# A reordered input projection: pooled inputs and values in the first pairs, the pooled path in eight steps, raw weights also in the tiles of the split of x

## The chip, the cores and the metric

The kernel runs on one core of one Trainium2 chip. The metric is the device time of one execution in microseconds (us). The engines are named as in the profile: PE is TensorE (PEld its weight loads), DVE is VectorE, ACT is ScalarE, POOL is GpSimd, SP is the engine that issues most DMAs. Each engine, and each engine's DMA queue, takes its instructions in order.

## The reference

One layer of a streaming encoder in float32, S = 1024 tokens, D = 1024, sandwich RMSNorms, input and output (1, 1024, 1024). What matters here is the first half:

```python
h = rms_norm(x, norm_mix_pre[l])
proj = h @ w_in[l]                       # 1024 x 4096: q, k, v, u (512 each), gates (2 x 1024)
q, k, v, u, gates = jnp.split(proj, splits, axis=-1)
y_a = chunk_band_attention(q, k, v, rel_bias[l]) @ w_attn_out[l]
y_b = multiscale_pool(u, w_pool_group[l], pool_scale[l]) @ w_pool_out[l]
g_a, g_b = jnp.split(jax.nn.sigmoid(gates + b_gate[l]), 2, axis=-1)
mix = (g_a * y_a + g_b * y_b) @ w_o[l]
x = x + rms_norm(mix, norm_mix_post[l])
f = conv_gated_ffn(rms_norm(x, norm_ffn_pre[l]), w_up[l], conv_w[l], conv_b[l], w_down[l])
x = x + rms_norm(f, norm_ffn_post[l])
```

`multiscale_pool` has four groups of 128 channels with trailing means over 2, 4, 8 and 16 tokens (computed by 1, 2, 3 and 4 doublings), minus the token, then a 128 x 128 matrix and a scale per channel. The FFN goes up to 2 x 2816, through a causal convolution of width 3, and down.

## The kernel before

A float32 operand is split into a high and a low part (`split`, L79: a cast on ACT gives `wh`, a subtraction on DVE gives `wl`), and each product is three matmuls of these parts (L85). A product of a 512 x 128 weight block with 512 tokens is twelve matmuls 128x512.

**In-projection (L367 to L738).** The 32 blocks of 128 output channels are computed in 16 pairs (`IN_PAIRS`), each by a Strassen-like scheme of seven products per pair of blocks (class `Pair`). It is done in two parts. First, while x still comes in, p1 and p2 of all pairs run on the tokens' first half (loop `for n in range(5, NP)`, with smaller weight loads `w12`); p1's results go to memory as `c1_d`. Then pairs are "turned" (`turn`): their whole raw weights are loaded (`load_win`, 1 MB, tile `win`), and `run_pair` runs p6, p3 and p7 of the pair, p5 of the next, and p4 of the pair. Per pair:

- four weight sums s1 (L203, `first`), s2, s4, s3 (L207 to L209, `sums`). The engine is the pair's `eng`: DVE for pairs 0 to 2, POOL for the others.
- `X_i<-c1b,R` on DVE (L254) seeds a bank; `u2` (L261) and `p5` (L218) are copies on ACT that hand a bank's content on.
- the evictions d(0,1) after p3 and d(1,1) after p7 are additions on DVE (L528); p4 cannot begin in p7's bank before d(1,1) has read it. d(0,0) and d(1,0) need no addition.
- `put` sends the result on: gates get their sigmoid on ACT (L521) and are stored by ACT's queue; pooled inputs u are stored to `u_d`; values wait in `vds` and are transposed by PE (`values`, `vps` L542, split into `vt`); q and k are split (`hl`, L499, L500) and stored.

**Pooled path.** `pooled_load` brings a group's u back as [128, 1024]. `pooled_path` (L554) does the doublings (`pl`, copies L560 and additions L561), the mean and the subtraction (L565 to L567) and the split into `pdh` (ACT) and `pdl` (DVE) at one place; `pooled_out` (L573), one pair later, loads and splits `wg`, makes the products `mxp` (six matmuls), scales them (`mo`) and splits into the tiles `mx`. In the kernel before the pooled groups are at pairs 6, 8, 10 and 12.

**Tiles.** "raw" has 6 buffers (raw weights, at first x, later `mx`), "S" and "o" 4 each, "hl" 2. x split in high and low (`XRh`, `XRl`) lies in tiles of the pool `hd` that attention's heads use later (tags `qk0`, `qk1`, `kl`, `bt`); p1 and p2 are its only readers.

**What follows.** `split_yb` loads and splits the first two weight blocks of the pooled out-projection during the last pair; then come that projection, attention, the out-projection and the FFN. The FFN's up-projection uses the same `Pair` class on 22 pairs u0 to u21 (`pair_up`, and `ahead` for u2 to u4, whose p1 and p2 run early); its sums are on POOL but for u5.

What sets the order: the program is written in the order of the loop; a scheduler then places each engine's instructions by priority (position in the program, raised by `tc.high_priority()`) and readiness. DMA queues take their issues in order.

Of the kernel before, what the change touches and what calls it, by code (L numbers as in the profile page):

```python
# [10 lines left out]
F32 = mybir.dt.float32  # L11
F32R = mybir.dt.float32r
AF = mybir.ActivationFunctionType
ALU = mybir.AluOpType
# [3 lines left out]
P = 128  # L18
S = 1024
# [15 lines left out]


IN_PAIRS = (
    [(16 + m, 24 + m) for m in range(4)]
    + [(12, 13), (14, 15)]
    + [(8, 9), (10, 11)]  # L40
    + [(16 + m, 24 + m) for m in range(4, 8)]
    + [(0, 4), (1, 5), (2, 6), (3, 7)]
)

# [2 lines left out]
def trunk(ctx, tc, xn, xt, w_first, w_in, cols, gain_pre, bias, w_ao, w_pg, w_po, w_o, gains, w_up, w_dn, out):  # L47
    nc = tc.nc
# [26 lines left out]
    def raw_tile(name):  # L75
        return rawp.tile([P, 2048], F32, tag="raw", name=name)
# [290 lines left out]
    with ExitStack() as ph:  # L367
# [4 lines left out]
        raws = {}  # L372

        def load_win(pi):
            raws[pi] = raw_tile(f"win{pi}")
            nc.sync.dma_start(raws[pi], w_in[pi])

        def half_tile(name):
# [2 lines left out]
        def out_tile(f, dt=F32):  # L381
            return tmp.tile([P, 512], dt, tag="hl", name=f)
# [117 lines left out]
                V.scalar_tensor_tensor(lo, src, scale, hi.bitcast(F32), ALU.mult, ALU.subtract)  # L500
            eng.dma_start(dst.rearrange("a p n -> p a n"), d.bitcast(F32))

        vds = []

        def put(fb, f, t, d, src):

# [17 lines left out]
        def evict_in(fb):  # L524
            def evict(f, t, ps, add):
                d = half_tile(f"d{fb[f]}_{t}")
                if add is not None:
                    V.tensor_tensor(d, ps, add, ALU.add)  # L528
                elif fb[f] < 16:
                    A.copy(d, ps)  # L530
                if (f, t, fb) == (1, 1, IN_PAIRS[-4]):

                    A.activation(warm, d[:, :1], AF.Exp, scale=0.0)
                put(fb, f, t, d, ps if add is None else d)
            return evict
# [13 lines left out]
        def pooled_load(m):  # L549
            u = tmp.tile([P, S], F32, tag="o", name=f"u{m}", bufs=4)  # L550
            nc.sync.dma_start(u, u_d[m])
            return u

        def pooled_path(m, u):  # L554
            w = POOL_WINDOWS[m]
            src = u
            step = 1
            while step < w:
                dst = tmp.tile([P, S], F32, tag="o", bufs=4, name=f"pl{m}_{step}")
                V.tensor_copy(dst[:, :step], src[:, :step])  # L560
                V.tensor_tensor(dst[:, step:], src[:, step:], src[:, :S - step], ALU.add)  # L561
                src = dst
                step *= 2
            e = w - 1
            V.tensor_tensor(src[:, :e], src[:, :e], cv[:, C_INV:C_INV + e], ALU.mult)  # L565
            V.tensor_tensor(src[:, :e], src[:, :e], u[:, :e], ALU.subtract)
# [4 lines left out]
            return m, hi, lo  # L571

        def pooled_out(m, hi, lo):  # L573
# [12 lines left out]

        first_yb = []

        def split_yb(m):
            wr = tmp.tile([P, 4, P], F32, tag="S", name=f"wr_yb{m}", bufs=4)  # L590
            (G if m else nc.sync).dma_start(wr, w_po[m])
            first_yb.append(split_w(wr, f"yb{m}", V))

        pairs = []

        def begin(n):
            p = Pair(None, T, psp, tmp, f"i{n}", None, 6, V if n < 3 else G)
# [114 lines left out]
        pair.p4(False)  # L714
        third.p5()
        nxt.p4(False)
        pair, pd = third, None
        for pi in range(2, NP):
            fb = IN_PAIRS[pi]
            for n in (pi + 1, pi + 2):  # L720
                if n < NP and n not in raws and (pi < 9 or n == pi + 1):
                    load_win(n)
            if pi in (7, 11):
                for x in range(2):
                    mx[x].append(rawp.tile([P, 2, S], F32R, tag="raw", name=f"mx{x}{pi}"))
            m = {6: 0, 8: 1, 10: 2, 12: 3}.get(pi)
            u = None if m is None else pooled_load(m)
            after = turn(pi + 1) if pi + 1 < NP else None
            run_pair(pair, after,
                     {"p6": lambda: split_yb(0), "p7": lambda: split_yb(1)} if after is None else (), True)  # L730
            pair = after
            values()
            if pd is not None:
                pooled_out(*pd)
            pd = None if u is None else pooled_path(m, u)
            if pi == 14:
                load_head(0)
                load_head(1)  # L738


    atp = ExitStack()
# [386 lines left out]
    with ExitStack() as ph:  # L1128
# [21 lines left out]

        def pair_up(g):

            return Pair(raws[g], Tu, psp, tmp, f"u{g}", evict_up(g), 4, V if g == 5 else G)

        def operand(name, src):
            hi, lo = Tu[name] = [Tp.tile([P, 4, 512], F32R, tag=name + x, name=name + x) for x in "hl"]
# [8 lines left out]

        def ahead(g):

            p = Pair(None, Tu, psp, tmp, f"u{g}", None, 4)
            w = Tp.tile([P, 1024], F32, tag=("T3h", "T3l", "T4h")[g - 2], name=f"w12_{g}")
            nc.sync.dma_start(w, w_up[g][:, :1024])  # L1170
            p.begin(w, p.pt("p1"))

            def evict(f, t, ps, add):
                d = p.pt("p2")
                A.copy(d, ps)
                nc.sync.dma_start(e_d[0, g - 2], d)
# [348 lines left out]
```

## Time and profile before

| | |
|---|---|
| runs | 1257.35, 1259.21, 1260.66 us; median 1259.21 |
| profiled execution | 1259.18 us, its span 1257.4 us |
| PE busy | 1231.3 us, 98% |
| DVE busy | 932.1 us, 74% |
| ACT busy | 663.5 us, 53% |
| POOL busy | 300.5 us, 24%, 236 instructions |

The span is cut into 40 slices in the page; the busy tenths of PE and DVE and PE's clock:

```profile
PE   8999999998899999999999999999999999999997
DVE  4897336758588877854799877676666676899968
PEclk9999999999999999999999999999999999999999
```

A slice is 31.4 us. The in-projection takes slices 1 to 11 (to about 345 us), attention follows, the FFN's up-projection begins at about 620 us. In slices 10 and 11 PE has 8. A timeline row gives start, duration, engine, line, operation, names (out<-in), sizes, and in brackets the engine's idle time before it with what ended it; a row of waits gives total, times and longest; a row of groups gives count | busy time, mean ns | idle time.

### The profile page before, as it was taken

The page shows a single profiled execution, that of the slowest core. Times are in us where ns is not written, and L with a number is a line of the kernel's source. Part 1 is how long each engine was busy: PE and PEld are TensorE (multiplying, and loading weights), DVE is VectorE, ACT ScalarE, POOL GpSimd, SP SyncE. Part 2 cuts the span into 40 slices and gives each one's busy share as a digit, 9 for nine tenths or more (in the row PEclk, how much of TensorE's full clock was granted, in tenths as well). Part 3 has the DMA queues.
Part 4 walks back from the last instruction along what each step waited for, and adds up shares of the span by engine and source line. Part 5 has one row for each costly group of instructions (what it writes and reads, how often), then busy time and mean ns, then how long its engine had stood idle before and what let it go on. Part 6 is the DMA issues. An engine that isn't in the chain of part 4 may idle for free.

```text
span 1257.4 us, 16281 instructions
## 1 busy us (share of the span) xinstructions
PE 1231.3 (98%) x5732; PEld 1021.9 (81%) x5732; DVE 932.1 (74%) x1497; ACT 663.5 (53%) x1170; POOL 300.5 (24%) x236
## 2 busy tenths in 40 slices
PE   8999999998899999999999999999999999999997
PEld 6888887787688998888888788888888888888886
DVE  4897336758588877854799877676666676899968
ACT  5664434544477774433464555555555454444553
POOL 0001433416244456000003443333333310000000
PEclk9999999999999999999999999999999999999999
DMA  9978423536787646512333332221221215902003
GB/s 334 322 245 310 142 101 108 215 119 228 235 291 266 207 150 253 204 68 84 118 121 143 128 136 97 95 101 51 101 101 43 101 67 204 390 17 101 34 1 135
DMA packets 63794, 193.85 MB, mean 154 GB/s; under 512 B 6048, under 2 KB 6688, under 8 KB 58592
## 3 DMA queue, kind: packets, MB, share of 16 engines
q1 hardware_dynamic: 55568, 176.29, 40.1%
q10 hardware_dynamic: 7056, 12.59, 2.7%
q0 software_dynamic: 1088, 3.93, 0.8%
q8 instruction: 45, 0.74, 0.2%
q14 instruction: 37, 0.30, 0.1%
HBM read 139.84 MB, written 52.95 MB: 153 GB/s over the span
## 4 chain that ended last, share of the span: by engine, by line
PE 82%; DVE 12%; issue 3%; ACT 2%; DMA 2%; SPq 0%; DVEq 0%; POOL 0%; ACTq 0%
PE X_u L85 16%; PE X_i L85 10%; PE Y_u L85 8%; PE X L85 7%; PE wops L1080 7%; PE Y_i L85 7%; PE Z_u L85 4%; PE y L85 4%; PE Y L85 3%; PE ybp L85 3%; PE f L881 3%; PE tp L856 2%; PE first L452 2%; PE Z_i L85 2%; DVE hc L1204 1%
## 5 line engine op out<-in xcount | busy, mean ns | idle before, releaser
L1204 DVE SCALAR_TENSOR_TENSOR hc<-hu,cv,hc 128x1022 f32<-128x1022 f32 (+1 forms) x88 | 120.1, 1366 | 30.2 <-ACT hc L1199 29.8
L79 ACT CAST wh_u<-s_u 128x512 fp32r<-128x512 f32 x88 | 54.3, 618 | 86.3 <-PE Y_u L85 43.5
L79 DVE TENSOR_TENSOR wl_u<-s_u,wh_u 128x512 fp32r<-128x512 f32 x88 | 65.4, 746 | 34.0 <-ACT wh_u L79 34.0
L79 ACT CAST wh_i<-s_i 128x512 fp32r<-128x512 f32 x64 | 39.6, 621 | 73.2 <-PE Y_i L85 21.3
L79 DVE TENSOR_TENSOR wl_i<-s_i,wh_i 128x512 fp32r<-128x512 f32 x64 | 50.2, 791 | 35.5 <-ACT wh_i L79 35.5
L203 POOL TENSOR_TENSOR s_i<-win 128x512 f32<-128x512 f32 x13 | 23.7, 1821 | 174.5 <-DVE wl_i L79 134.9
L79 ACT CAST wh_u<-wup 128x512 fp32r<-128x512 f32 x60 | 37.2, 621 | 48.7 <-PE X_u L85 25.8
L1199 ACT ACTIVATE hc<-hu,cv 128x1024 f32<-128x1024 f32 x44 | 54.7, 1244 | 10.8 <-DVE hu L1148 9.9
L207 POOL TENSOR_TENSOR s_u<-s_u,wup 128x512 f32<-128x512 f32 x19 | 27.1, 1425 | 133.5 <-DVE wl_u L79 122.5
L203 POOL TENSOR_TENSOR s_u<-wup 128x512 f32<-128x512 f32 x19 | 34.0, 1791 | 72.9 <-DVE wl_u L79 72.9
L835 POOL TENSOR_SCALAR pe<-pe,st 128x640 f32<-128x640 f32 (+4 forms) x58 | 40.7, 705 | 44.0 <-DVE st L833 29.6
L79 DVE TENSOR_TENSOR ptl<-tp,pth 128x512 fp32r<-128x512 f32 (+3 forms) x80 | 42.8, 552 | 7.8 <-ACT pth L79 7.2
L831 ACT ACTIVATE pe<-sm,st 128x640 f32<-128x640 f32 (+2 forms) x64 | 44.3, 694 | 7.7 <-DVE st L829 7.5
L1209 ACT ACTIVATE hc<-hc 128x1024 f32<-128x1024 f32 x22 | 23.4, 1063 | 45.5 <-DVE hc L1204 45.5
L209 POOL TENSOR_TENSOR s_u<-wup 128x512 f32<-128x512 f32 x19 | 40.1, 2110 | 26.5 <-DVE wl_u L79 26.5
L79 ACT CAST pth<-tp 128x512 fp32r<-128x512 f32 (+3 forms) x80 | 36.3, 475 | 15.9 <-PE tp L856 11.0
L79 DVE TENSOR_TENSOR wl_u<-wup,wh_u 128x512 fp32r<-128x512 f32 x60 | 43.2, 721 | 0.7
L85 PE MATMUL ybp<-mx,wh_yb 128*128 128x512 f32 x128 | 43.4, 412 | 0.0
L829 DVE CUSTOM_DVE_ANT_0 sm<-pst,bt 128x640 f32<-128x640 f32 (+2 forms) x64 | 40.7, 652 | 3.1 <-issue 1.7
L881 PE MATMUL f<-pth,vv 128*128 128x256 f32 x144 | 36.5, 286 | 0.0
L881 PE MATMUL f<-ptl,vv 128*128 128x256 f32 x144 | 36.5, 287 | 0.0
L856 PE MATMUL tp<-ident,pe 128*128 128x128 f32 x240 | 35.4, 275 | 0.2
(518 smaller groups left out, 4158.7 us busy)
## 6 DMA issues: line engine op xcount, KB each, us to landing
wup<-in_w_up SPq DMA_DIRECT2D x22, 1024.0 KB, 5.0
win<-in_w_in SPq DMA_DIRECT2D x16, 1024.0 KB, 5.5
g_d<-hc SPq DMA_DIRECT2D x20, 512.0 KB, 2.6
a<-g_d SPq DMA_DIRECT2D x8, 1024.0 KB, 10.9
b<-in_w_dn SPq DMA_DIRECT2D x8, 1024.0 KB, 12.8
sig_d<-d ACTq DMA_DIRECT2D x28, 256.0 KB, 2.4
w<-in_w_in SPq DMA_DIRECT2D x12, 512.0 KB, 6.8
x<-in_xn SPq DMA_DIRECT2D x8, 512.0 KB, 8.5
```

The costliest lines, as they stand in the source:

```text
L79: return A.copy(hi, src), (eng or V).tensor_tensor(lo, src, hi.bitcast(F32), ALU.subtract)
L85: nc.tensor.matmul(ps, a[i], b[i], start=start and i == 0 and p == 0, stop=stop and i == n - 1 and p == 2, skip_group_check=True,)
L203: self.eng.tensor_tensor(self.s1, self.w21, self.w22, ALU.add)
L209: self.eng.tensor_tensor(self.s3, self.w11, self.w21, ALU.subtract)
L829: V.tensor_tensor_reduce(so, sv, bv, -1.0, 3e38, ALU.add, ALU.min, st[:, 0:1])
L831: A.activation(pe[:, :n], sm[:, :n], AF.Exp, scale=-1.0, bias=st[:, 0:1], accum_out=st[:, 1:2])
L835: (V if 4 * h + J in (0, 1, 31) else G).tensor_scalar(pe[:, :n], pe[:, :n], st[:, 2:3], 1.0, ALU.mult, ALU.mult)
L856: nc.tensor.transpose(tp[:, c * P:(c + 1) * P], pe[:, b * P:(b + 1) * P], ident)
L881: nc.tensor.matmul(fo, vv[:, kb, e].rearrange("p a d -> p (a d)"), t[:, s], start=s == slots[0] and x == 0, stop=s == slots[-1] and x == 1)
L1080: nc.tensor.matmul(ps[:, 512 * c:512 * c + 512], a[k // 4][:, k % 4, sl], wo[k][b][:, 512 * c:512 * c + 512], start=k == 0 and x == 0, sto ...
L1199: A.activation(c, hu, AF.Identity, scale=cv[:, C_CW + 88 + b:C_CW + 89 + b], bias=cv[:, C_CB + b:C_CB + b + 1])
L1204: V.scalar_tensor_tensor(c[:, n:], hu[:, :S - n], cv[:, w:w + 1], c[:, n:], ALU.mult, ALU.add)
```

## The change

Four things are changed.

1. The order of pairs: pooled inputs, values, all gates, then q and k.
2. The pooled path is cut into steps (`pooled_sums`, `pooled_split`, `pooled_out`) which are put at the ends of pairs 4 to 11, one or two per pair, each issued behind the pair's eviction d(1,1); that eviction gets high priority.
3. The raw weights of pairs 6, 8, 10 and 12 go into the tiles of the split of x (`qk0`, `qk1`), so that weights are always loaded two pairs ahead. The loads for `split_yb` go to SP and stand, with the loads of heads 0 and 1, before the last pair.
4. Weight sums: DVE for pairs 3 to 11 (POOL before; nine pairs with four sums each), and in the FFN for u2, u3, u4 and u6 (sixteen sums).

```diff
 IN_PAIRS = (
-    [(16 + m, 24 + m) for m in range(4)]
-    + [(12, 13), (14, 15)]
+    [(12, 13), (14, 15)]
     + [(8, 9), (10, 11)]
-    + [(16 + m, 24 + m) for m in range(4, 8)]
+    + [(16 + m, 24 + m) for m in range(8)]
     + [(0, 4), (1, 5), (2, 6), (3, 7)]
 )
...
         def load_win(pi):
-            raws[pi] = raw_tile(f"win{pi}")
+            if pi in (6, 8, 10, 12):
+                raws[pi] = hd.tile([P, 2048], F32, tag=f"qk{pi // 2 % 2}", name=f"win{pi}")
+            else:
+                raws[pi] = raw_tile(f"win{pi}")
             nc.sync.dma_start(raws[pi], w_in[pi])
...
                 if add is not None:
-                    V.tensor_tensor(d, ps, add, ALU.add)
+                    with tc.high_priority() if f == t == 1 else nullcontext():
+                        kept[f, t] = V.tensor_tensor(d, ps, add, ALU.add)
...
-        def pooled_path(m, u):
-            w = POOL_WINDOWS[m]
-            src = u
-            step = 1
-            while step < w:
+            pooled[m] = u, u, 1
+
+        def pooled_sums(m, end):
+            u, src, step = pooled[m]
+            while step < end:
                 dst = tmp.tile([P, S], F32, tag="o", bufs=4, name=f"pl{m}_{step}")
                 V.tensor_copy(dst[:, :step], src[:, :step])
                 V.tensor_tensor(dst[:, step:], src[:, step:], src[:, :S - step], ALU.add)
                 src = dst
                 step *= 2
+            pooled[m] = u, src, step
+
+        def pooled_split(m):
+            w = POOL_WINDOWS[m]
+            pooled_sums(m, w)
+            u, src, _ = pooled[m]
...
-        first_yb = []
+        first_yb, wr_yb = [], []
+
+        def load_yb(m):
+            wr_yb.append(out_tile(f"wr_yb{m}").rearrange("p (k c) -> p k c", k=4))
+            nc.sync.dma_start(wr_yb[m], w_po[m])
 
         def split_yb(m):
-            wr = tmp.tile([P, 4, P], F32, tag="S", name=f"wr_yb{m}", bufs=4)
-            (G if m else nc.sync).dma_start(wr, w_po[m])
-            first_yb.append(split_w(wr, f"yb{m}", V))
+            first_yb.append(split_w(wr_yb[m], f"yb{m}", V))
...
-            p = Pair(None, T, psp, tmp, f"i{n}", None, 6, V if n < 3 else G)
+            p = Pair(None, T, psp, tmp, f"i{n}", None, 6, V if n < 12 else G)
...
+        steps = {
+            4: lambda: pooled_split(0),
+            5: lambda: (pooled_out(0), pooled_sums(1, 4)),
+            6: lambda: pooled_split(1),
+            7: lambda: (pooled_out(1), pooled_sums(2, 4)),
+            8: lambda: pooled_split(2),
+            9: lambda: (pooled_out(2), pooled_sums(3, 8)),
+            10: lambda: pooled_split(3),
+            11: lambda: pooled_out(3),
+        }
         for pi in range(2, NP):
...
-                if n < NP and n not in raws and (pi < 9 or n == pi + 1):
+                if n < NP and n not in raws:
                     load_win(n)
-            if pi in (7, 11):
+            if pi in (5, 9):
...
-            m = {6: 0, 8: 1, 10: 2, 12: 3}.get(pi)
-            u = None if m is None else pooled_load(m)
+            if pi in (4, 5, 7, 9):
+                pooled_load({4: 0, 5: 1, 7: 2, 9: 3}[pi])
             after = turn(pi + 1) if pi + 1 < NP else None
+            if after is None:
+                load_yb(0)
+                load_yb(1)
+                load_head(0)
+                load_head(1)
             run_pair(...)
...
-            if pd is not None:
-                pooled_out(*pd)
-            pd = None if u is None else pooled_path(m, u)
-            if pi == 14:
-                load_head(0)
-                load_head(1)
+            if pi in steps:
+                with tc.issue_after(kept[1, 1].ins):
+                    steps[pi]()
...
         def pair_up(g):
-            return Pair(raws[g], Tu, psp, tmp, f"u{g}", evict_up(g), 4, V if g == 5 else G)
+            return Pair(raws[g], Tu, psp, tmp, f"u{g}", evict_up(g), 4, V if g < 7 else G)
...
         def ahead(g):
-            p = Pair(None, Tu, psp, tmp, f"u{g}", None, 4)
+            p = Pair(None, Tu, psp, tmp, f"u{g}", None, 4, V)
```

DVE around d(1,1) beside the sums of pooled group 3, first before, in the turn of pair 13 (the result for block 5, a k block; d5_1 is its d(1,1)). The numbers in the names `i13`, `pl3_4` are the pair, and the group with its doubling; the last number of a name is the buffer's.

```order
L561 TENSOR_TENSOR pl3_4_2577<-pl3_2_2574 128x1020
L528 TENSOR_TENSOR d1_1_2632<-Y_i13_2530,u2_i13_2596 128x512
L560 COPY pl3_8_2580<-pl3_4_2577 128x8
L561 TENSOR_TENSOR pl3_8_2580<-pl3_4_2577 128x1016
L528 TENSOR_TENSOR d5_1_2654<-X_i13_2597,p5_i13_2531 128x512
L565 TENSOR_TENSOR pl3_8_2580<-pl3_8_2580,cv_76 128x15
L567 SCALAR_TENSOR_TENSOR pl3_8_2580<-pl3_8_2580,u3_2453 128x1009
L566 TENSOR_TENSOR pl3_8_2580<-pl3_8_2580,u3_2453 128x15
```

And now, in the turn of pair 10 (a gate pair; the lines are the changed file's, d30_1 is the d(1,1)):

```order
L533 TENSOR_TENSOR d22_1_2286<-Y_i10_2175,u2_i10_2250 128x512
L78 TENSOR_TENSOR wl_6_i11_2374<-s2_i11_2310,wh_6_i11_2373 128x512
L533 TENSOR_TENSOR d30_1_2306<-X_i10_2251,p5_i10_2176 128x512
L563 COPY pl3_8_2354<-pl3_4_2241 128x8
L564 TENSOR_TENSOR pl3_8_2354<-pl3_4_2241 128x1016
L78 TENSOR_TENSOR wl_3_i11_2391<-s4_i11_2311,wh_3_i11_2390 128x512
L574 TENSOR_TENSOR pl3_8_2354<-pl3_8_2354,cv_76 128x15
L576 SCALAR_TENSOR_TENSOR pl3_8_2354<-pl3_8_2354,u3_2103 128x1009
```

The last doubling has moved from between the two evictions to behind both, and three pairs earlier in the program.

ACT around the cast `pdh` of pooled group 1, before, in the turn of pair 9:

```order
L521 ACTIVATE d28_0_2043<-X_i8_1943,cv_76 128x512
L522 DMA sig_d_70<-d28_0_2043 128x512
L79 CAST pdh1_2055<-pl1_2_2049 128x1024
L261 COPY u2_i9_2063<-X_i9_2064 128x512
L79 CAST wh_4_i9_2148<-win9_1778 128x512
```

And now, in the turn of pair 6:

```order
L525 DMA sig_d_70<-d26_1_1784 128x512
L78 CAST pdh1_1835<-pl1_2_1719 128x1024
L217 COPY p5_i7_1795<-Y_i7_1794 128x512
L78 CAST wh_7_i7_1887<-s3_i7_1790 128x512
L78 CAST wh_5_i8_1915<-s1_i8_1845 128x512
```

What stands behind the cast is now the copy of p5 and no longer that of u2.

SP's queue around the load of the first block for `split_yb`, before; the second block was on POOL's queue:

```order
L362 DMA kl1_2855<-k_d_67 64x1024
L501 DMA k_d_67<-hl_2795 128x2x512
L591 DMA wr_yb0_2882<-in_w_po 128x512
L786 DMA vv0_3009<-v_d_68 128x2x1024
L798 DMA sgb0_2987<-sig_d_70 128x1024
```

And now:

```order
L379 DMA win14_2496<-in_w_in 128x2048
L601 DMA wr_yb0_2846<-in_w_po 128x512
L632 DMA c1b_14_2616<-c1_d_74 128x512
L601 DMA wr_yb1_2848<-in_w_po 128x512
L504 DMA q_d_66<-hl_2540 128x2x512
L356 DMA qk0_2850<-q_d_66 128x1024
```

Both blocks stand ahead of the first stores of q and k, where before the one load came behind the last of them.

More of the change, by code (lines that the diff above doesn't have):

```diff
@@ L501, in store_split @@
             eng.dma_start(dst.rearrange("a p n -> p a n"), d.bitcast(F32))
-        vds = []
+        vds, kept = [], {}
         def put(fb, f, t, d, src):
@@ L551, in pooled_load @@
             nc.sync.dma_start(u, u_d[m])
-            return u
-        def pooled_path(m, u):
-            w = POOL_WINDOWS[m]
-            src = u
-            step = 1
-            while step < w:
+            pooled[m] = u, u, 1
+        def pooled_sums(m, end):
+            u, src, step = pooled[m]
+            while step < end:
                 dst = tmp.tile([P, S], F32, tag="o", bufs=4, name=f"pl{m}_{step}")
@@ L570, in pooled_path, with pooled_out @@
             split(hi, lo, src)
-            return m, hi, lo
-        def pooled_out(m, hi, lo):
+            pooled[m] = hi, lo
+        def pooled_out(m):
+            hi, lo = pooled.pop(m)
             wg = tmp.tile([P, P], F32, tag="S", bufs=4, name=f"wg{m}")
@@ L716, in trunk @@
         nxt.p4(False)
-        pair, pd = third, None
+        pair, pooled = third, {}
+        steps = {
[8 more added lines that the diff above has]
+        }
         for pi in range(2, NP):
-            fb = IN_PAIRS[pi]
             for n in (pi + 1, pi + 2):
-                if n < NP and n not in raws and (pi < 9 or n == pi + 1):
+                if n < NP and n not in raws:
                     load_win(n)
-            if pi in (7, 11):
+            if pi in (5, 9):
                 for x in range(2):
                     mx[x].append(rawp.tile([P, 2, S], F32R, tag="raw", name=f"mx{x}{pi}"))
-            m = {6: 0, 8: 1, 10: 2, 12: 3}.get(pi)
-            u = None if m is None else pooled_load(m)
+            if pi in (4, 5, 7, 9):
+                pooled_load({4: 0, 5: 1, 7: 2, 9: 3}[pi])
             after = turn(pi + 1) if pi + 1 < NP else None
+            if after is None:
[3 more added lines that the diff above has]
+                load_head(1)
             run_pair(pair, after,
```

## The prediction

> **What bounds the kernel now.** I read the busy shares and the chain of the page first, then the waits of TensorE (PE) for the stage that the change rewrites, then windows of that stage, then single rows around each wait.
>
> ```profile
> PE 1231.3 (98%) x5732; PEld 1021.9 (81%) x5732; DVE 932.1 (74%) x1497; ACT 663.5 (53%) x1170; POOL 300.5 (24%) x236
> PE 82%; DVE 12%; issue 3%; ACT 2%; DMA 2%; SPq 0%; DVEq 0%; POOL 0%; ACTq 0%
> 125.00:195.00 70.00, 70.00 (x311) 57.95 (x310) 27.03 (x41) 27.13 (x46) 28.67 (x21) 1.00 0.33 113
> 237.00:251.00 14.00, 14.00 (x55) 11.39 (x56) 10.43 (x15) 8.01 (x15) 7.75 (x5) 0.88 0.36 129
> 293.00:308.00 15.00, 12.28 (x51) 9.80 (x50) 15.00 (x20) 4.57 (x8) 8.10 (x5) 0.92 0.82 275
> 323.00:345.00 22.00, 18.46 (x76) 14.53 (x75) 9.35 (x18) 8.48 (x18) 3.41 (x11) 0.92 0.80 275
> ```
>
> A windows row is from:to, length, busy time (count) of PE, its weight load, DVE, ACT, POOL, then PE's granted clock, DMA share, GB/s. PE is the bound, and no matmul is added or removed, so only PE's idle time and its slow clock can be won: 1257.4 - 1231.3 = 26.1 us idle, plus what the clock costs inside busy time. From 125 to 195 us PE is full at clock 1.00. The losses stand where pooled path, values and gates meet, 195 to 345 us. PE's waits there (us in total, times, longest):
>
> ```profile
> PE Y_i L85 <- ACT wh_i L79: 3.5, 1, 3.5
> PE X_i L85 <- DVE d L528: 3.3, 2, 2.7
> PE X_i L85 <- ACT u_i L261: 2.5, 2, 2.0
> PE vps L542 <- DVE vt L79: 1.1, 1, 1.1
> PE Y_i L85 <- DVE wl_i L79: 0.8, 1, 0.8
> ```
>
> Together 11.2 us. After the three longest, twelve matmuls run partly at half clock; from the chain (start, us, piece), with an undisturbed product last:
>
> ```profile
> 236.84 4.61 PE X_i L85 x12
> 305.94 4.45 PE X_i L85 x12
> 332.47 4.78 PE Y_i L85 x12
> 244.20 2.72 PE X_i L85 x12
> ```
>
> The excess over 2.72 is 1.89 + 1.73 + 2.06 = 5.7 us. The pool from which this change can draw is 11.2 + 5.7 = 16.9 us. Why each happens:
>
> ```profile
> 235.26 1.04 ACT L79 CAST pdh<-pl 128x1024 fp32r<-128x1024 f32 x1 [4.74 <-DVE pl L566]
> 236.21 0.58 ACT L261 COPY u_i<-X_i 128x512 f32<-128x512 f32 x1
> 303.40 0.68 DVE L528 TENSOR_TENSOR d<-Y_i,u_i 128x512 f32<-128x512 f32 x1
> 304.00 0.16 DVE L560 COPY pl<-pl 128x8 f32<-128x8 f32 x1
> 304.07 1.21 DVE L561 TENSOR_TENSOR pl<-pl 128x1016 f32<-128x1016 f32 x1
> 305.20 0.68 DVE L528 TENSOR_TENSOR d<-X_i,p_i 128x512 f32<-128x512 f32 x1
> 331.28 0.62 ACT L79 CAST wh_yb<-wr_yb 128x512 fp32r<-128x512 f32 x1 [3.74 <-DMA wr_yb<-in_w_po]
> 283.35 1.29 POOL L203 TENSOR_TENSOR s_i<-win 128x512 f32<-128x512 f32 x1 [19.74 <-DMA win<-in_w_in]
> ```
>
> At 236.84 ACT's queue is held for 4.74 us by pooled group 1's cast, and the copy of u that PE waits for stands behind it. At 305.94 the sums of group 3 stand between and ahead of the two evictions d on a DVE that was busy for the whole 15 us (the window 293:308); d began at 305.20, long after its product. The shorter waits for d (0.6) and u (0.5) stand beside other groups' pooled work. At 332.47 the first weight block of the next projection was fetched too late. The 0.8 us is a weight sum that waited for its own raw weights.
>
> **The change, part by part.**
>
> (a) *Pooled path in eight steps, over gate pairs.* A turned pair is five products of 2.72, 13.6 us. From 125 to 195 us, 70/13.6 = 5.1 such pairs, DVE is busy 27.03, or 5.3 us a pair. To this come four weight sums from POOL; one more 128x512 operation holds DVE for 304.00 - 303.40 = 0.60, so 2.4. The heaviest step is group 2's output with the first three sums of group 3: three copies and adds at 305.20 - 304.00 = 1.20, 3.6, and three small operations, about 1.4. Sum 12.7 us, against 13.6 plus six matmuls of group 2 (half a product, 1.36): 15.0. It fits, though with little over. What decides is d(1,1), which must be finished while the next product runs, 2.72 us: it now has priority and the steps are issued behind it, so at worst one long operation (1.2) and its own 0.7 stand before it, 1.9 us. The cast pdh now stands ahead of the copy of p5 and not of u; the copy is needed only by the next d(1,1), four products later. Removed: 2.7 + 0.6 + 2.5 in waits, and 1.89 + 1.73 of clock: 9.4 us.
>
> (b) *Values in early pairs whose sums are on DVE.* The wait of 1.1 us before vps:
>
> ```profile
> 215.23 0.66 PE L542 MATMUL vps<-ident,d 128*128 128x128 f32 x4 [1.11 <-DVE vt L79]
> 212.19 0.69 DVE L79 TENSOR_TENSOR wl_i<-s_i,wh_i 128x512 fp32r<-128x512 f32 x1 [1.01 <-ACT wh_i L79]
> 212.80 1.79 DVE L254 TENSOR_TENSOR X_i<-c1b,R 128x512 f32<-128x512 f32 x1
> 212.28 1.75 POOL L209 TENSOR_TENSOR s_i<-win 128x512 f32<-128x512 f32 x1
> 195.00:223.00 28.00, 26.89 (x130) 21.78 (x129) 18.93 (x28) 14.60 (x26) 7.72 (x5) 1.00 0.44 156
> ```
>
> The DVE operation from 212.80 took 1.79, where the like one before it took 0.69, and ended 0.56 after POOL's sum ended (214.03): POOL's sum held it back 1.1 us, and vt behind it. Without POOL's sum that goes: 1.1. So a sum moved costs DVE 0.60 and takes away up to 1.1; net it costs between +0.60 and -0.5 each. I count it at nothing in the pairs, where DVE has idle time.
>
> (c) *The block's load and the raw weights.* The load wr_yb was issued at 324.26 and took 7.00:
>
> ```profile
> 324.26 7.00 DMA wr_yb<-in_w_po
> ```
>
> It now stands on SP's queue two to three pairs earlier, some 30 us ahead of need, into a tile of group 3's weights; behind it on SP wait the q and k stores and two head loads, and win15, which is needed a pair later (13.6 us, against some 7 for a load). That returns 3.5 + 2.06. Raw weights always two ahead return the 0.8.
>
> (d) *Function tables on ACT.* With gates no longer first, sigmoid falls between the squares and the root of the norm, so the table is loaded three times there and not once:
>
> ```profile
> 44.00 1.28 ACT L521 ACT_TABLE_LOAD   x1
> PE rps L471 <- DVE bc L468: 0.2, 1, 0.2
> ```
>
> Two more at 1.28 are 2.56 us on ACT. They delay the norm's root, and through DVE's bc PE's transposes rps; these already waited 0.2, but now stand one product later in PE's order. Bounds: 0 if that product (2.72) covers it, 2.56 if nothing does. I take 0.3, near the row's own 0.2.
>
> (e) *FFN up-projection, sixteen sums from POOL to DVE.*
>
> ```profile
> 640.00:700.00 60.00, 59.77 (x264) 49.13 (x263) 59.37 (x66) 32.28 (x46) 16.37 (x9) 1.00 0.45 158
> L1204 DVE SCALAR_TENSOR_TENSOR hc<-hu,cv,hc 128x1022 f32<-128x1022 f32 (+1 forms) x11 | 17.7, 1626 | 0.3
> L79 DVE TENSOR_TENSOR wl_u<-s_u,wh_u 128x512 fp32r<-128x512 f32 x16 | 12.9, 819 | 0.0
> L79 DVE TENSOR_TENSOR wl_u<-wup,wh_u 128x512 fp32r<-128x512 f32 x5 | 4.4, 899 | 0.0
> 695.17 1.27 DVE L1204 SCALAR_TENSOR_TENSOR hc<-hu,cv,hc 128x1023 f32<-128x1023 f32 x1
> PE X_u L85 <- DVE hu L1148: 1.0, 2, 0.8
> ```
>
> DVE is full there (59.37 of 60), so cover is gone and the price counts. Nine sums add 9 x 0.60 = 5.4 us. Against it: L1204 takes 1626 ns in the mean and 1.27 us undisturbed, 11 x 0.36 = 3.9; the two wl groups stand 0.13 and 0.21 over 0.69, 2.1 + 1.0. Up to 7.0 us of slowing, all beside POOL's sums, goes away. Net 1.6 us less for DVE. PE's waits there are 1.0 in all; I take back 0.3. Bounds: 1.0 won; or, with no slowing removed, 5.4 - 0.6 of DVE's idle time = 4.8 lost.
>
> **Sum.** 9.4 (a) + 1.1 (b) + 5.6 + 0.8 (c) = 16.9; I leave 1.0 of it as new short waits, since the heaviest step leaves only 2.3 us of DVE. Less 0.3 (d), plus 0.3 (e): 15.9. The profiled execution took 1259.18 us (span 1257.4); the median of the runs is 1259.21, practically the same, so the result stands for it: 1243.3, say 1243.5.
>
> One rule speaks against this sum. The Trainium skill, "TensorE: Matmul & The Clock Gate", Part 1, says that the clock falls to half after at least one idle window of about 3.4 us. By that rule only the wait of 3.5 could have cost clock, the 1.89 and 1.73 would have another cause and stay, and the sum would end at 1247. This trace disagrees: PE's granted clock fell after waits of 2.0 and 2.7 as well, and not after 1.1 (the window 195:223 has 1.00). I go by the trace: a wait of 2 us costs about 4. That the slow matmuls stay for another reason gets 0.05 of the forecast's chance below; 1243.5 + 3.6 = 1247 is its upper end.
>
> **Rivals.**
>
> 1. *DVE late in some steps* (0.13). The steps with three adds miss the 2.72 us. Each such stall costs what 305.94 did, 2.7 + 1.73 = 4.5. Two of eight: 1252.5. For it: DVE has no idle time from 293 to 308 today. Against: priority, and the sum of 12.7 in 15.0.
> 2. *Pooled stalls only move* (0.08): a cast or wgl now blocks another copy on ACT, as pdh did. Then (a) and (b) return nothing, (c) returns 6.4: 1253.
> 3. *FFN's DVE becomes the bound* (0.10): the moved sums cost 4.8 there, and the slowing stays because others of POOL's sums remain: 1243.5 + 0.3 + 4.8 = 1248.6.
> 4. *Slower* (0.06): d(1,1) late by 2 us or more in each step that ends with sums or a split. It decides from four stalls of 4.5 upward, 18 against the 15.9 won; six give 1243.5 + 27 = 1270. For it: a full DVE; against: between 125 and 195 us DVE is busy 39%.
>
> **How the numbers follow.** The forecast, 1240 to 1247, has 0.57: full return and 1.0 in the FFN give 1259.2 - 17.9 = 1241.3, and a little more with fewer slowed operations; 2.56 for the tables and another 1 of waits give 1247. The remaining 0.06 is for gains and losses that cancel, near 1257. What a measurement can tell is about 0.3%, 3.8 us: faster means below 1255.4. Forecast and rivals 1 to 3 lie there, 0.88; same 0.06; slower 0.06. The range that leaves out the slow cases and half of the odd ones is 1239.5 to 1254.
>
> **What would show it.** Right: PE's waits of 195 to 345 us are gone but for pieces below 1 us, PE's clock reads 1.00 from 31 us to the end of the in-projection, no idle ACT before wh_yb, POOL at about 52 sums fewer (236 instructions to about 184), the phase ending some 16 us earlier. Wrong in (a): a row X_i with idle time from d, and twelve matmuls over 4 us. Wrong in (d): PE waiting for bc by more than 0.5 near 53 us. Wrong in (e): X_u or Y_u waiting for hu or wl_u, summing over 2 us between 620 and 760.

## The result and the profile after

The changed kernel takes 1239.18 us (median of six runs, 1238.54 to 1240.40), the kernel before 1259.14 (six runs, 1257.35 to 1260.97). The ratio is 0.9842, interval 0.983 to 0.9855: 20.0 us faster. Forecast were 15.9 us, 1243.5, in a range from 1239.5: the direction was right, the gain a fifth too small, and the time lies just below the range. Of the eight runs of one experiment below, that with only the sums moved, one took 1535.56 us at a granted clock of 0.75; its time is the median of the seven others.

The page after, busy shares and shares of the chain:

```profile
PE 1222.6 (99%) x5732; PEld 1018.1 (82%) x5732; DVE 947.8 (77%) x1549; ACT 667.8 (54%) x1172; POOL 211.6 (17%) x183
PE 90%; DVE 7%; issue 1%; ACT 1%; DMA 0%; POOL 0%; DVEq 0%; SPq 0%; POOLq 0%; ACTq 0%
```

PE has the same 5732 matmuls. POOL issues 183 instructions in place of 236, DVE 52 more. The chain, of which DVE held 12%, is 90% PE. PE's waits from the start to 345 us, all of them:

```profile
PE first L455 <- ACT w0s L78: 6.3, 1, 6.3
PE rps L474 <- DVE bc L471: 0.2, 1, 0.2
PE tp L880 <- POOL pe L859: 0.2, 1, 0.2
```

The five rows of 11.2 us are gone, and nothing has come in their place. The windows of the two kernels, from 125 us to about the end of the in-projection, before first, and then the FFN's two windows after:

```profile
125.00:342.00 217.00, 205.87 (x890) 167.17 (x889) 125.52 (x174) 97.80 (x167) 80.07 (x53) 0.98 0.48 164
125.00:330.00 205.00, 205.00 (x919) 169.67 (x918) 143.11 (x226) 105.35 (x181) 28.62 (x28) 1.00 0.51 176
623.00:683.00 60.00, 60.00 (x266) 49.71 (x265) 59.31 (x78) 32.54 (x45) 0.00 (x0) 1.00 0.46 159
683.00:743.00 60.00, 60.00 (x266) 49.66 (x266) 50.74 (x57) 32.57 (x49) 11.49 (x8) 1.00 0.34 127
```

Before, PE idled 217.00 - 205.87 = 11.1 us at a mean clock of 0.98; after, it is full at 1.00. In the FFN, too, PE is full (60.00 twice, where it had 59.77 and 59.06), beside a DVE as busy as before: 59.31.

Adding up, from the starts of the matmuls, what lies beyond their usual spacing (0.227 us for 128x512), PE lost 18.2 us from 125 us to the end of the in-projection before and 0.2 after; in the 140 us of the FFN's first part 2.2 before and 0.1 after; from 31 to 125 us 0.4 before and 0.7 after. That is 18.0 + 2.1 - 0.3 = 19.8, the gain of the medians. (The two profiled spans differ by 20.4. Ahead of 31 us, where the first matmuls of each kernel are twice as far apart, PE lost 2.8 us before and 1.6 after.)

### The profile page after: what moved, and what is told of

The parts are those of the page before. It is cut to its first block, busy times and chain, and to the rows that moved or that the text cites. A ratio compares the mean times of both kernels' runs of the same rounds, so it can differ in the third digit from the quotient of the medians.

```text
span 1237.0 us, 16222 instructions
## 1 busy us (share of the span) xinstructions
PE 1222.6 (99%) x5732; PEld 1018.1 (82%) x5732; DVE 947.8 (77%) x1549; ACT 667.8 (54%) x1172; POOL 211.6 (17%) x183
## 4 chain that ended last, share of the span: by engine, by line
PE 90%; DVE 7%; issue 1%; ACT 1%; DMA 0%; POOL 0%; DVEq 0%; SPq 0%; POOLq 0%; ACTq 0%
PE X_u L84 19%; PE X_i L84 12%; PE Y_u L84 10%; PE Y_i L84 8%; PE X L84 7%; PE wops L1104 7%; PE Z_u L84 4%; PE y L84 4%; PE Y L84 4%; PE ybp L84 3%; PE f L905 2%; PE tp L880 2%; PE first L455 2%; PE Z_i L84 2%; DVE b L1394 1%; DVE a L1394 1%
## 5 line engine op out<-in xcount | busy, mean ns | idle before, releaser
L1228 DVE SCALAR_TENSOR_TENSOR hc<-hu,cv,hc 128x1022 f32<-128x1022 f32 (+1 forms) x88 | 115.5, 1314 | 27.8 <-ACT hc L1223 27.7
L78 DVE TENSOR_TENSOR wl_u<-s_u,wh_u 128x512 fp32r<-128x512 f32 x88 | 62.3, 711 | 33.9 <-ACT wh_u L78 33.9
L78 DVE TENSOR_TENSOR wl_i<-s_i,wh_i 128x512 fp32r<-128x512 f32 x64 | 44.7, 700 | 21.9 <-ACT wh_i L78 16.9
L202 POOL TENSOR_TENSOR s_i<-win 128x512 f32<-128x512 f32 x4 | 6.2, 1561 | 259.4 <-DVE wl_i L78 248.3
L202 POOL TENSOR_TENSOR s_u<-wup 128x512 f32<-128x512 f32 x15 | 25.7, 1713 | 139.3 <-DVE wl_u L78 139.3
L78 ACT CAST pth<-tp 128x512 fp32r<-128x512 f32 (+3 forms) x80 | 36.3, 475 | 15.9 <-PE tp L880 11.0
L206 POOL TENSOR_TENSOR s_u<-s_u,wup 128x512 f32<-128x512 f32 x15 | 19.4, 1293 | 102.3 <-DVE wl_u L78 99.6
L208 POOL TENSOR_TENSOR s_u<-wup 128x512 f32<-128x512 f32 x15 | 32.2, 2145 | 23.5 <-DVE wl_u L78 23.5
```

The lines of the kernel that those rows point to most:

```text
L78: return A.copy(hi, src), (eng or V).tensor_tensor(lo, src, hi.bitcast(F32), ALU.subtract)
L202: self.eng.tensor_tensor(self.s1, self.w21, self.w22, ALU.add)
L208: self.eng.tensor_tensor(self.s3, self.w11, self.w21, ALU.subtract)
L1228: V.scalar_tensor_tensor(c[:, n:], hu[:, :S - n], cv[:, w:w + 1], c[:, n:], ALU.mult, ALU.add)
```

## The experiments

Times are medians. Each experiment undoes one thing in the changed kernel, or does one thing in the kernel before; the last two measure DVE's room. The kernel before, on the same chip each time, took 1259.25 to 1259.61 us, and 1261.39 beside the last two, which were run once.

**FFN sums back on POOL.**

```diff
-            return Pair(..., evict_up(g), 4, V if g < 7 else G)
+            return Pair(..., evict_up(g), 4, V if g == 5 else G)
-            p = Pair(None, Tu, psp, tmp, f"u{g}", None, 4, V)
+            p = Pair(None, Tu, psp, tmp, f"u{g}", None, 4)
```

> The changed kernel with the FFN's sixteen weight sums back on POOL. Theory (the gain that the prediction missed lies partly in the FFN, where waits read as 1.0 us cost about 2): 1.7 to 2.3 us slower than the changed kernel's 1239.18, so about 1241, and waits of X_u for hu are back between 605 and 745 us. Rival (the FFN gave 0.3 as forecast, the rest is the clock at the start): 1239.2 to 1239.6.

Measured: 1241.42, ratio 0.986 (0.9845 to 0.9875), 2.2 slower than the changed kernel. Its waits of the FFN's first part, its window, and DVE's three groups of the changed kernel (623 to 683 us):

```profile
PE X_u L84 <- DVE hu L1172: 1.1, 2, 0.9
625.00:685.00 60.00, 59.76 (x264) 49.18 (x263) 59.37 (x66) 31.10 (x43) 18.52 (x9) 1.00 0.44 153
L1228 DVE SCALAR_TENSOR_TENSOR hc<-hu,cv,hc 128x1022 f32<-128x1022 f32 (+1 forms) x12 | 15.2, 1276 | 0.0
L78 DVE TENSOR_TENSOR wl_u<-s_u,wh_u 128x512 fp32r<-128x512 f32 x16 | 10.8, 682 | 0.0
L78 DVE TENSOR_TENSOR wl_u<-wup,wh_u 128x512 fp32r<-128x512 f32 x7 | 4.7, 683 | 0.0
```

The FFN's part is worth 2.2 and not 0.3. The means fell from 1626, 819 and 899 ns to 1276, 682 and 683: all slowing is gone, and DVE does 78 instructions in the time of 66. These agree with the full relief that the prediction worked out (7.0 us against 5.4 added); what it got wrong was how much of that PE would feel.

**In-projection sums of pairs 3 to 11 back on POOL.**

```diff
-            p = Pair(None, T, psp, tmp, f"i{n}", None, 6, V if n < 12 else G)
+            p = Pair(None, T, psp, tmp, f"i{n}", None, 6, V if n < 3 else G)
```

> The changed kernel with the in-projection's sums of pairs 3 to 11 back on POOL. Theory (POOL's sums hold DVE back by 1.1 us each, and a DVE with the pooled steps can't bear that): two to four stalls, 2 to 8 us slower, 1241 to 1247, and DVE's wl_i mean near 0.85 us instead of 0.70. Rival (order and steps alone remove the stalls): within 0.5 us of 1239.2.

Measured: 1238.66, ratio 0.9836 (0.9819 to 0.9852): the rival. DVE's group of weight sums from 125 to 330 us, this kernel first, then the changed one:

```profile
L78 DVE TENSOR_TENSOR wl_i<-s_i,wh_i 128x512 fp32r<-128x512 f32 x53 | 43.6, 826 | 27.6 <-ACT wh_i L78 27.6
L78 DVE TENSOR_TENSOR wl_i<-s_i,wh_i 128x512 fp32r<-128x512 f32 x53 | 37.3, 705 | 20.8 <-ACT wh_i L78 15.8 <-PE vps L547 2.6 <-PE mxp L84 2.3
```

The slowing is back (826 ns against 705) and costs nothing. Held-back DVE operations cost no time in this stage, where DVE was busy 134.24 of the 205 us; in the FFN, where it was busy 59.37 of 60, the sums back on POOL cost 2.2.

**No priority for d(1,1), steps not issued behind it.**

```diff
-                    with tc.high_priority() if f == t == 1 else nullcontext():
+                    with nullcontext():
...
-                with tc.issue_after(kept[1, 1].ins):
+                with nullcontext():
                     steps[pi]()
```

> The changed kernel without the priority of d(1,1) and without issuing the steps behind it. Theory (the eviction's place decides): one to three stalls of PE behind d at the ends of pooled pairs, 1 to 9 us slower. Rival (the steps are small enough wherever they stand): within 0.5 us.

Measured: 1239.23, ratio 0.9842 (0.9827 to 0.9856). The rival again: no stall.

**Block load as before.**

```diff
         def split_yb(m):
-            first_yb.append(split_w(wr_yb[m], f"yb{m}", V))
+            wr = tmp.tile([P, 4, P], F32, tag="S", name=f"wr_yb{m}", bufs=4)
+            (G if m else nc.sync).dma_start(wr, w_po[m])
+            first_yb.append(split_w(wr, f"yb{m}", V))
```

> The changed kernel with the two blocks of the pooled out-projection loaded as before, in the last pair, one by SP and one by POOL. Theory (that load alone made the last stall and its half clock): 3.7 + 2.1 = 5.8 us slower, 1245, one wait of Y_i for wh_i near 313 us and twelve matmuls of 4.6 to 4.8 us behind it. Rival (the queue is now free, the load lands in time): 1239 to 1240.

Measured: 1240.17, ratio 0.9849 (0.9834 to 0.9864), close to the rival; PE does not wait for the block in its profile. The load's issue and the cast in its timeline:

```profile
308.82 0.41 SPq L601 DMA_DIRECT2D wr_yb<-in_w_po  x1
315.05 0.62 ACT L78 CAST wh_yb<-wr_yb 128x512 fp32r<-128x512 f32 x1 [2.85 <-DMA wr_yb<-in_w_po]
```

ACT still waits 2.85 us for the block, and PE does not: the load went out ahead of the last k store, where in the kernel before it stood behind it. With the old code the new surroundings let it pass in time. By the starts of its matmuls PE lost 0.1 us from 125 us to the end of the in-projection, no more than in the changed kernel, and ahead of 31 us 3.0 against 1.6; so this load does not account for the 1.0 us of the medians.

**Pooled path in one step per group.**

```diff
-            5: lambda: (pooled_out(0), pooled_sums(1, 4)),
+            5: lambda: pooled_out(0),
...
-            9: lambda: (pooled_out(2), pooled_sums(3, 8)),
+            9: lambda: pooled_out(2),
```

> The changed kernel with each pooled group's sums, mean and split in one step (pairs 4, 6, 8, 10), the output in the next pair. Theory (the pieces must be short): group 3, some 8 us of DVE in one pair beside 7.7 us of its own, makes one or two stalls with half clock, 3 to 9 us slower. Rival (over gate pairs with d(1,1) first, DVE has room anyway): within 0.5 us of 1239.2.

Measured: 1239.02, ratio 0.9842 (0.9825 to 0.9858): no stall, and the cutting into steps alone is worth nothing.

**Raw weights only in the raw tiles.**

```diff
-            if pi in (6, 8, 10, 12):
-                raws[pi] = hd.tile([P, 2048], F32, tag=f"qk{pi // 2 % 2}", name=f"win{pi}")
-            else:
-                raws[pi] = raw_tile(f"win{pi}")
+            raws[pi] = raw_tile(f"win{pi}")
...
-                if n < NP and n not in raws:
+                if n < NP and n not in raws and (pi < 9 or n == pi + 1):
```

> The changed kernel with all raw weights in the raw tiles, loaded two ahead only up to pair 8 as before. Theory (a late raw weight cost only the 0.8 us before pair 13): 0.5 to 1.5 us slower, POOL's sum s1 of a late pair waiting for win. Rival (DVE's sums need their weights earlier than POOL's did, in the middle of the loop): two or more stalls, over 4 us slower.

Measured: 1240.41, ratio 0.9854 (0.9839 to 0.9868), 1.2 slower, with a wait of Y_i for wl_i (0.6 us) and one of X_i for wh_i (0.2): the theory, about the 0.8 that the prediction had for it.

**The old order of pairs, all else new** (steps in pairs 7 to 14).

```diff
 IN_PAIRS = (
-    [(12, 13), (14, 15)]
+    [(16 + m, 24 + m) for m in range(4)]
+    + [(12, 13), (14, 15)]
     + [(8, 9), (10, 11)]
-    + [(16 + m, 24 + m) for m in range(8)]
+    + [(16 + m, 24 + m) for m in range(4, 8)]
```

> The changed kernel with the old order of pairs; the pooled steps then stand in pairs 7 to 14, the last ones over q and k pairs. Theory (the order matters because q and k pairs have four splits more on ACT and DVE and their sums on POOL): stalls return in pairs 12 to 14, 3 to 10 us slower. Rival (steps and DVE sums suffice in any order): within 1 us of 1239.2.

Measured: 1245.77, ratio 0.9896 (0.9881 to 0.9911), 6.6 slower. SP's row for the loads, what SP waited for before it, and the stall:

```profile
314.21 1.23 SPq L602 DMA_DIRECT2D wr_yb<-in_w_po  x2
SPq L602 <- PE mxp L85: 2.1, 1, 2.1
322.70 0.80 PE L85 MATMUL Y_i<-B22h,wh_i 128*128 128x512 f32 x1 [5.57 <-ACT wh_i L79]
```

The time is in the expected band, but not for the expected reason. No stall stands behind the pooled path, though its last steps lie over q and k pairs. Nearly the whole loss is the block load and the half clock behind it: its tile is now that of the group weights, group 3 comes late in this order, the load waits for that group's products (`mxp`), and it leaves at 314.21 where the changed kernel sends it at 271.90.

**Only the sums, in the kernel before** (`V if n < 3 else G` to `V if n < 12 else G`).

> The kernel before with one thing changed: the in-projection's sums of pairs 3 to 11 on DVE. Theory (POOL's sums were only part of the stalls): the vps wait of 1.1 goes, the rest stays, 1 to 3 us faster than before's 1259.14. Rival 1 (the contention was the cause of most stalls): 6 to 11 us faster. Rival 2 (DVE is too full beside the undivided pooled path): 2 to 8 us slower.

Measured: 1255.81, ratio 0.9975 (0.9965 to 0.9986), 3.8 faster, a little more than the theory's 1 to 3. The waits for vt and the long one for u are gone; that for d stays at 3.2 in all, that at the block load grew from 3.5 to 4.9.

**Only the order, in the kernel before** (the first hunk of the diff).

> The kernel before with the new order of pairs and nothing else: undivided pooled path at pairs 6, 8, 10 and 12, POOL's sums, late block load, FFN as before. Theory (with the new order three groups fall on gate pairs, and each other part is a second cure of the same stalls): the in-projection loses at most 4 to 8 us in place of 18, 1245 to 1250; what is left stands at pair 12 or after and at the block load. Rival (the order alone moves the stalls; the steps are what removes them): 1254 to 1259.

Measured: 1255.12, ratio 0.9961 (0.9946 to 0.9976), 4.4 faster, outside the theory's band and inside the rival's. Its waits:

```profile
PE Y_i L84 <- ACT wh_i L78: 4.8, 2, 4.2
PE X_i L84 <- DVE d L527: 3.3, 2, 2.7
PE Y_i L84 <- DVE wl_i L78: 0.9, 1, 0.9
PE X_i L84 <- ACT u_i L260: 0.6, 1, 0.6
```

Groups 0 to 2 cost less (the waits for u of 2.0 and for vt of 1.1 are gone), but group 3 still stands at pair 12, over q and k pairs, and so does the block load.

**The order, and the undivided pooled path two pairs earlier.**

```diff
-            if pi in (7, 11):
+            if pi in (5, 9):
...
-            m = {6: 0, 8: 1, 10: 2, 12: 3}.get(pi)
+            m = {4: 0, 6: 1, 8: 2, 10: 3}.get(pi)
```

> As the run before it, and the undivided pooled groups moved to pairs 4, 6, 8 and 10, so that none touches a q or k pair. Theory (where the pooled path stands is the whole cause in the in-projection): at most 2.5 us of PE's loss left there, 1241 to 1244 with the FFN's 2.2 still to pay. Rival (POOL's sums and the undivided path together stall PE where either alone does not): two stalls or more, over 1247.

Measured: 1248.25 (1246.21 to 1251.42), ratio 0.9909 (0.9887 to 0.993), 11.3 faster. Its waits in the in-projection:

```profile
PE Y_i L84 <- ACT wh_i L78: 2.0, 1, 2.0
PE Y_i L84 <- DVE wl_i L78: 0.8, 1, 0.8
PE X_i L84 <- DVE d L527: 0.5, 1, 0.5
```

Place alone takes away the long stall at d and the one at the block load, though that load is as before. One of 2.0 and two short ones remain; the profile's loss in the stage is 6.0 us of 18.2. The waits of 2.0 and 0.8 follow each other at 254.93 and 256.49 us, and with the half clock behind them they are 4.9 of these 6.0. The rows ahead of them:

```profile
250.53 1.77 POOL L202 TENSOR_TENSOR s_i<-win 128x512 f32<-128x512 f32 x1 [18.92 <-DMA win<-in_w_in]
252.42 1.03 ACT L78 CAST pdh<-pl 128x1024 fp32r<-128x1024 f32 x1
254.28 0.60 ACT L78 CAST wh_i<-s_i 128x512 fp32r<-128x512 f32 x1
```

POOL's sum waited for its raw weights and ended at 252.30; its cast stood on ACT behind the pooled cast `pdh` and a sigmoid until 254.28. Neither theory held in full: place is the greater part, and raw weights, a sum on POOL and the undivided path, of which none alone cost the changed kernel more than 1.2 us, meet in the stall that is left.

**Only steps and priority, in the kernel before** (pairs 7 to 14, old order).

> The kernel before, in the old order of pairs, with the pooled path in steps (pairs 7 to 14) and the priority of d(1,1), and nothing else changed. Theory (steps and priority cure the stalls behind d and u, not the block load): the 2.9 and 2.1 waits with their half clock go, 6 to 10 us faster than 1259.1, a stall of 4 to 6 us at the block load stays. Rival (steps beside POOL's sums over q and k pairs are no better): within 3 us of before.

Measured: 1251.27, ratio 0.9936 (0.9913 to 0.9958), 8.3 faster. Its waits in the in-projection:

```profile
PE Y_i L85 <- ACT wh_i L79: 4.4, 2, 2.2
PE X_i L85 <- DVE d L530: 1.7, 1, 1.7
PE Y_i L85 <- DVE wl_i L79: 0.5, 1, 0.5
```

The amount is as expected. The stalls are others: shorter, and only one of the three longer ones threw the clock down (below). That one, the first wait of 2.2 (it ended at 295.70), is not the pooled path's: the raw weights of a late pair were issued at 285.72, landed 7.8 us later, and POOL's first sum of them began at 293.67. The wait for d (1.7) is what is left of the pooled path's stalls, and the second wait for wh_i is the block load.

**Only the block load early, in the kernel before.**

```diff
-            wr = tmp.tile([P, 4, P], F32, tag="S", name=f"wr_yb{m}", bufs=4)
-            (G if m else nc.sync).dma_start(wr, w_po[m])
...
+            if pi == 13:
+                load_yb(0)
+                load_yb(1)
```

> The kernel before with the two blocks of the pooled out-projection loaded by SP into the tiles of the group weights, issued ahead of the last q and k stores; nothing else changed. Theory (the late load is the cause of the last stall in the old order): that stall and its half clock go, 5.6 us faster, 1253.5. Rival (the queue is full there, or the tile is free too late): 0 to 2 us faster.

Measured: 1253.36, ratio 0.9948 (0.9932 to 0.9964), 6.2 faster; the wait for wh_i is gone, all others stay, within 0.4 us each. This is about the 5.6 of the prediction's step (c).

**DVE's room** (two kernels, other pairs in the second): the addition of d(1,1) is done several times over.

```diff
+                        for _ in range(again.get(IN_PAIRS.index(fb), 0) if f == t == 1 else 0):
+                            V.tensor_tensor(d, ps, add, ALU.add)
```

> The changed kernel with the addition of d(1,1) repeated 5, 6, 7, 8 and 9 times more in pairs 2, 4, 6, 8 and 10 (the same result is written again), so that PE waits for it some 1.2, 1.8, 2.4, 3.0 and 3.6 us. Theory (the clock is decided in windows of 3.41 us on a fixed grid, and falls for one window when the window before had about 2 us or more without matmuls): half clock after the waits of 2.4 to 3.6 where most of the wait lies in one window, at the next multiple of 3.41 from the clock's first rise, and none where the wait is cut in two by a boundary. Rival 1 (a whole window of 3.4 must be idle): none but perhaps after 3.6. Rival 2 (every wait of 2 us or more): after 2.4, 3.0 and 3.6 always.

> As s1_ladder, in pairs 3, 5, 7, 9 and 11 with 6, 6, 7, 7 and 8 repeats, waits of some 1.8, 1.8, 2.4, 2.4 and 3.0 us at other places of the grid. Same theories: on the grid theory waits of equal length differ by where the boundary falls; on rival 2 they do not.

Measured: 1242.87 and 1241.49, one run each, on a chip on which the kernel before took some 2 us longer too. They say nothing of the clock, for PE waited 0.7 us at most: the order that the scheduler gave PE puts other products ahead of p4. The first kernel's window:

```profile
125.00:330.00 205.00, 204.15 (x906) 166.55 (x905) 161.06 (x251) 101.58 (x175) 27.34 (x25) 1.00 0.50 172
```

They show something else. 35 further additions, 35 x 0.60 = 21 us of DVE (161.06 against 143.11 busy here, though the window then holds less of attention), cost PE 0.85 us of idle time; by the starts of the matmuls PE lost 3.0 us in this stage, where the changed kernel loses 0.2, and as much in the second kernel. So 2.8 us for 21: that much room was left in the pairs that rival 1 feared for.

## Why the prediction was right or wrong

*What bounds the kernel.* Right for the in-projection: PE's idle time and clock were its pool, and nearly all of it came back (18.2 us lost before, 0.2 after). The size of the pool was short. It was read off printed waits, 11.2 us, and a printed wait begins at the modelled end of the last matmul. The row before the wait of 1.96:

```profile
234.50 0.39 PE L85 MATMUL Y_i<-B22h,wl_i 128*128 128x512 f32 x1
```

Matmuls follow each other every 0.227 us, so the wait was 236.84 - 234.50 - 0.23 = 2.1. Seven waits of this stage are short by 0.16 each, 1.1 us. With the half clock that makes 18.0 in place of 16.9.

*(a) Pooled path.* Forecast 9.4, of which 1.0 in reserve. The stalls went fully. The reason given, small steps behind a d(1,1) that goes first, is not what is needed: undoing the priority (1239.23), the steps (1239.02) or the sums (1238.66) costs nothing. Steps alone in the old order gave 8.3, the new place alone 11.3, and the longest stall that was left in either stood at late raw weights. Each cures most of the pooled stalls by itself, and in the changed kernel any one of them can be missed. Undone all together, with the rest of the change, at the new place (1248.25), they cost 9.1, of which the FFN has 2.2; pairs of them were not tried.

*(b) Values.* The wait for vt is gone with the sums alone and with the order alone; here, too, one cure is enough.

*(c) Block load and raw weights.* 5.6 forecast for the load; 6.2 measured by itself in the kernel before. In the changed kernel its undoing costs 1.0 by the medians and nothing by the profile. 0.8 forecast for the raw weights, 1.2 measured in the changed kernel; with the steps alone and with the place alone late raw weights took part in a stall of 2.0 to 2.2 us and its half clock.

*(d) Function tables.* 0.3 forecast. The three loads stand where they were expected:

```profile
41.27 1.28 ACT L524 ACT_TABLE_LOAD   x1
47.87 1.28 ACT L312 ACT_TABLE_LOAD   x1
50.10 1.28 ACT L524 ACT_TABLE_LOAD   x1
```

PE's wait for bc is 0.2 in the changed kernel, as before, and up to 0.8 in experiments with the new order (0.8 with the FFN's sums on POOL, 0.6 without priority). But it is 0.6 with only the block load early, too, in the old order with one load there, so what the two further loads cost is not shown; 0 to 0.6 us fits what was taken.

*(e) FFN.* The step that failed most, a term mis-sized: 0.3 taken, 2.2 measured, by the undoing (1241.42 against 1239.18). The prediction set PE's printed waits, 1.0, as the upper bound and took a third of it. The window that it quoted had 0.23 idle, and the next 60 us, not quoted, another 0.94. The longest of these waits in the kernel before:

```profile
706.34 0.39 PE L85 MATMUL Y_u<-T1h,wl_u 128*128 128x512 f32 x1
707.54 0.50 PE L85 MATMUL X_u<-T4h,wh_u 128*128 128x512 f32 x1 [0.81 <-DVE hu L1148]
707.88 0.40 PE L85 MATMUL X_u<-T4l,wh_u 128*128 128x512 f32 x1
```

The starts lie 1.20 and 0.34 apart in place of 0.227 twice: 1.08 us lost where 0.81 is printed. With the like one of 0.23, and a third at 740.65 that the list leaves out as too short, the three come to 2.0 us. A bound on what PE can win is its spacing, not its list of waits.

*The sum.* Missing were 1.0 of reserve that nothing used, 1.1 of wait ahead of the printed starts, 1.9 in the FFN: 4.0, which with 15.9 gives 19.9. The bottom of the range rested on the same short pool, and so lay 0.3 us above the median.

*The rivals.* None came. DVE late in some steps was answered by the additions repeated (2.8 us of PE for 21 us of DVE). Pooled stalls that only move were seen in none of the experiments that keep the new place with the steps or sums; with the undivided path and POOL's sums the cast `pdh` did hold back a weight's cast. The FFN's DVE did not become the bound.

*The clock.* The rule of the Trainium skill ("TensorE: Matmul & The Clock Gate", Part 1: half clock after at least one idle window of about 3.4 us) was put aside because 2.0 us of waiting sufficed. The prediction's own rule, a wait of 2 us costs about 4, does not hold either: see the end.

## What to carry to other kernels

Where several things go wrong in one stage, look first for another place for the work, one where the engine that it loads has room: here the order took the pooled path off the pairs with most splits, and then steps, priorities and the engine of the sums hardly mattered. Measure each part of a change undone and done alone, for parts can be second cures of one stall, and undoing one then shows zero though it is worth 8 us by itself. Size what an engine can win by the spacing of its instructions against the usual spacing, for a list of waits leaves out what lies under modelled ends and small gaps.

## What the runs showed of the hardware

The granted clock falls in steps of 3.41 us on a fixed grid. The kernel before, windows cut on that grid (PE's busy time first after the length; the clock is the third number from the end):

```profile
233.93:237.35 3.42, 1.46 (x7) 0.92 (x6) 2.92 (x6) 2.09 (x4) 0.00 (x0) 1.00 0.23 35
237.35:240.76 3.41, 3.41 (x9) 2.65 (x9) 3.41 (x7) 1.40 (x3) 1.62 (x2) 0.50 0.60 238
302.20:305.61 3.41, 1.02 (x5) 0.52 (x3) 3.41 (x7) 0.00 (x0) 0.00 (x0) 1.00 0.76 235
305.61:309.03 3.42, 3.10 (x7) 2.48 (x8) 3.42 (x8) 1.83 (x3) 1.58 (x1) 0.50 1.04 362
329.51:332.92 3.41, 0.45 (x2) 0.30 (x2) 0.99 (x2) 1.64 (x4) 0.00 (x0) 1.00 1.02 404
332.92:336.33 3.41, 3.41 (x9) 2.47 (x8) 1.60 (x3) 1.02 (x3) 0.00 (x0) 0.50 0.84 344
```

Between the three falls lie 68.26 and 27.31 us, 20.0 and 8.0 times 3.413. A fall comes at the end of a window in which PE was busy 1.46 us or less, lasts exactly one window in this kernel, and then the clock is full again. The early block load in the kernel before and the steps alone put the bound more closely:

```profile
234.93:238.34 3.41, 1.48 (x6) 1.24 (x7) 2.91 (x7) 2.77 (x5) 0.00 (x0) 1.00 0.48 132
238.34:241.76 3.42, 3.42 (x9) 2.65 (x8) 3.42 (x6) 1.34 (x2) 2.60 (x2) 0.50 0.49 194
313.60:317.02 3.42, 1.69 (x8) 1.09 (x8) 3.42 (x7) 2.21 (x5) 0.00 (x0) 1.00 0.49 121
317.02:320.43 3.41, 3.41 (x17) 2.80 (x16) 0.47 (x1) 1.32 (x3) 0.72 (x1) 1.00 0.84 262
320.43:323.84 3.41, 2.86 (x13) 2.05 (x11) 1.99 (x3) 2.47 (x6) 0.74 (x1) 1.00 1.02 340
323.84:327.26 3.42, 1.79 (x8) 1.38 (x9) 2.50 (x4) 2.62 (x5) 0.00 (x0) 1.00 1.02 363
327.26:330.67 3.41, 3.41 (x16) 2.81 (x15) 1.81 (x4) 1.26 (x2) 0.00 (x0) 1.00 0.89 320
```

1.48 us busy in a window threw the clock down, 1.69 and 1.79 did not. (Busy time is the profile's, with modelled ends.) The stall of 2.2 us that ended at 325.47 was cut in two by the boundary at 323.84 and cost no clock, one of 2.0 in one window did. So a stall of about 2 us costs 1.7 us of clock or nothing, by where it falls. The Trainium skill's Part 1 of that page also calls the window free-running and about 3.4 us; with that the traces agree (3.41). That the whole window must be idle they contradict: the clock fell with PE busy for 1.48 of 3.41 us. That only the grid decides was read from the stalls that happened; the two kernels meant to place stalls on purpose made none long enough.

A fall can last longer than one window. After the longest stalls at the block load, 5.57 us in the changed kernel with the old order and 4.91 with only the sums, it lasted two, 6.83 us. With only the sums:

```profile
327.64:331.05 3.41, 2.66 (x6) 2.04 (x7) 2.59 (x4) 2.22 (x5) 0.00 (x0) 0.50 0.88 358
331.05:334.47 3.42, 3.42 (x9) 2.64 (x8) 0.55 (x1) 0.62 (x1) 0.00 (x0) 0.50 0.07 26
```

With PE busy 2.66 us in the first of them the clock stayed at half; in the windows where it rose, PE had been busy 2.97 us or more (2.97 with only the order). So a long stall can cost a second slow window.
